# Spreading the second half's norm steps over later filler products at the border of two layers

## The chip, the cores and the metric

One core of a Trainium2 chip runs the whole program. The metric is the device time of one execution in microseconds (us); the time before is the median of three executions. The engines are named as in the profile: PE (TensorE, matrix products; PEld its weight loads), DVE (VectorE), ACT (ScalarE), POOL (GpSimd), and SP, whose queue issues every DMA.

## The reference: two decoder layers with a norm between them

The input is 1024 rows (positions) of width 1024. Layer 0 is retention, layer 1 stick-breaking attention; between them the residual stream is normed once and projected to a shared K and V, and normed again, with another gain, and projected to Q and a gate G:

```python
y = o @ ret_w_out[i]
h = h + rms_norm(y, ret_norm_post[i])
if i == N_A_LAYERS - 1:
    kv = rms_norm(h, kv_norm) @ w_kv
...
u = rms_norm(h, sb_norm_pre[j])
proj = u @ sb_w_in[j]
q, g = jnp.split(proj, [SB_QK_WIDTH], axis=-1)
```

Both projections read the same normed h; the two gains go into the weights. So at the border of the layers there is a chain: layer 0's last output y, its sum of squares over the width, `rms_norm` of y, h, the sum of squares of h, the scale of each row of h, and only then the operands of layer 1's projections.

## The kernel before: recorded operations, a planner, and filler products

**Halves.** Activations are kept transposed (width on the partitions). The 1024 positions are two halves of 512, t = 0 and t = 1. Layer 0 is finished for half 0 well before half 1, so at the border the first half's h is already normed and the second half's is not.

**Products.** Each pair of weight matrices of 1024x512 against the two halves is computed by a seven-product scheme of the Strassen kind (class `Group`, L1182): products 1 to 7, each of 4 chunks of 12 matmuls 128x128x512 into four PSUM banks, two `pma` and two `pmb` (or `pz` and `po`). A product's weight operand `whl` is a high and a low half in fp32r, made from raw fp32 weights `wraw`: ACT writes the high half (with the gain), DVE the low half, by `split` (L758). An activation operand is made in the same way: products 1 and 2 take theirs from half 0 alone, products 6, 5, 7, 3 and 4 need half 1 or both. There are three `whl` buffers, and a `whl` holds two of a product's four chunks.

**Groups and filler.** Layer 1's groups are K, Q, V0, G0, V1 and G1 (tables `kinds` and `early`, L1663 and L1664). Product 2 of the first five needs nothing of half 1 and is run ahead as filler, in that order; I call them the fillers K, Q, V0, G0 and V1. ACT copies each filler's four banks to SBUF (`f<-pma`, `f<-pmb`), and SP stores them (`s<-f`). Then come group K's product 1, product 6, 5, 7, 3, 4, and the other groups.

**The second half's chain**, recorded as side steps beside the fillers. In `a_post(1)` (L1054), `post` has 12 entries: `stat1` (four tiny matmuls, the sum over the width, then a power on POOL), `stat2` (a diagonal, `sgn`), `row` (one matmul `pz<-sgn,ones`, which spreads the scale along the positions), eight `add` steps, and `stat3`, which is `stat1` for h. An `add` step is three DVE instructions, `S<-S,gn,pz`, `S<-S,tab` and the sum of squares `acc<-acc,tab`, one ACT square `tab<-S`, and an SP store `h<-S`. `c_stats(1)` (L1117) is two entries: the diagonal and the row for h. `late` of `c_prep` (L1135) is 16 entries, four each of `rows` (half 1 times the row, four 128x512 or 128x1024 DVE instructions, and product 6's operand `xh`), `fives` (product 5's operand `qk`), `sevens` (product 7's, `oT`) and `rest` (products 3 and 4). `plain` is product 1's operands.

**What sets the order.** Nothing is issued when the Python code runs: `Recorder` notes every operation, `merge` (L693) spreads the side steps evenly over the chunks of the product they stand beside, and the record's order decides the order of the PE's work, whose turn a pooled buffer is, and the deadlines. `Plan` (L282) then goes over all recorded operations with durations per operation, and for every engine picks the next one by the time at which it can begin and the latest time at which it must be done for the PE; PE itself takes the recorded order, or a later operation among the next 100 where the recorded one would keep it waiting. The emitted program has a fixed order on each engine, and an engine that waits holds everything behind it. Because planning goes on to the end, a change in one place shifts the order in later places too.

Of the kernel before, what the change touches and what calls it, by code (L numbers as in the profile page):

```python
# [457 lines left out]
def trunk(ctx, tc, xT, wts, gains, trig, ident_in, cols, grow_in, out):  # L458
# [234 lines left out]
    def merge(main, *sides, nxt=None):  # L693


        done = [0] * len(sides)
        for i, m in enumerate(main):
            if nxt and nxt.pre and i == len(main) - 2:
                nxt.pre()
            m()  # L700
            for k, (steps, lead, tail) in enumerate(sides):
                n = len(main) - lead - tail
                upto = min(len(steps), len(steps) * max(0, i + 1 - lead) // n)
                while done[k] < upto:
                    steps[done[k]]()
                    done[k] += 1
# [20 lines left out]
    def diag(col):  # L727
        d = hl("sgn")
        for b in range(4):
            n = slice(128 * b, 128 * b + 128)  # L730
            V.tensor_scalar(d[:, 0, n], ident[:], col[:, b:b + 1], None, ALU.mult)
            V.scalar_tensor_tensor(d[:, 1, n], ident[:], col[:, b:b + 1], f32(d[:, 0, n]), ALU.mult, ALU.subtract)
        return d

    def short_row(col):
        d = S("sgn", [512])
        for b in range(4):
            n = slice(128 * b, 128 * b + 128)
            if b % 2:
                A_.activation(d[:, n], ident[:], AF.Copy, scale=col[:, b:b + 1])  # L740
            else:
                V.tensor_scalar(d[:, n], ident[:], col[:, b:b + 1], None, ALU.mult)
        return d

    def psum_row(d):
        p = PS("z")
        MM(p[:], ones[:], d[:], start=True, stop=True)
        return p

    def keep_row(d):  # L750
        p = PS("z")
        for l in range(2):
            MM(p[:], onesr[:], d[:, l, :], start=l == 0, stop=l == 1)
        row = S("acc", [512])
        A_.activation(row[:], p[:], AF.Copy)
        return row
# [297 lines left out]
    def a_post(t, y_d, acc, hold=None):  # L1054

        box = {}

        def stat1():
            box["col"] = rstd_col(acc[0])

        def stat2():
            box["d"] = short_row(box["col"]) if t else diag(box["col"])

        def row():
            box["rows"] = psum_row(box["d"]) if t else keep_row(box["d"])
            box["acc"] = S("acc", [512])

        def load(k):
            y, raw = box[k] = (hold[k % 4][:, k // 4], S("tab", [512])) if t else (S("vo", [512]), S("vo", [512]))
            if not t:  # L1070
                dma(y[:], y_d[k])
            dma(raw[:], xT[128 * k:128 * k + 128, HT * t:HT * t + HT])

        def add(k):
            c2, c = divmod(k, 2)
            y, raw = box[k]
            V.scalar_tensor_tensor(y[:], y[:], gcol(G_POST, k), box["rows"][:], ALU.mult, ALU.mult)
            (V if t else G).tensor_tensor(y[:], y[:], raw[:], ALU.add)
            dma(h_d[t][c2][:, 512 * c:512 * c + 512], y[:])

        def square(k):
            y, raw = box[k]
            if k == 0:
                A_.activation(box["acc"][:], y[:], AF.Square)
            else:
                A_.activation(raw[:], y[:], AF.Square)
                (V if t else G).tensor_tensor(box["acc"][:], box["acc"][:], raw[:], ALU.add)

        def stat3():
            colh[t] = rstd_col(box["acc"])  # L1090

        return [stat1, stat2, row] + in_turn(8, 3 if t else 0, load, add, square) + [stat3]
# [24 lines left out]
    def c_stats(t):  # L1117
        box = {}

        def dia():  # L1120
            box["d"] = short_row(colh[t]) if t else diag(colh[t])

        def row():
            rowh[t] = psum_row(box["d"]) if t else keep_row(box["d"])
        return [dia, row]
# [9 lines left out]
    def c_prep(hold):  # L1135

        X = Ctx()
        X.op = {n: [None] * 4 for n in range(1, 8)}
        X.raw = [None] * 4
        X.big = {}  # L1140

        def hi_lo(n, i, src, tag="xh"):
            if tag != "xh":
                if i == 0:
                    X.big[n] = S(tag, [4, 2, 512], F32R)
                x = X.big[n][:, i]
            else:
                x = hl("xh")
            X.op[n][i] = x
            split((x[:, 0, :], x[:, 1, :]), src)  # L1150

        def early(i, c):
            if c:
                X.raw[i] = h_rows(0, i)
            hi_lo(1 + c, i, X.raw[i][:, c])

        def rows(i):
            a, b = X.raw[i], h_rows(1, i, hold)
            t6 = S("f2", [512])
            V.tensor_tensor(a[:, 0], a[:, 0], b[:, 0], ALU.subtract)  # L1160
            V.scalar_tensor_tensor(t6[:], a[:, 0], -1.0, b[:, 1], ALU.mult, ALU.subtract)
            V.scalar_tensor_tensor(a[:, 1], t6[:], -1.0, a[:, 1], ALU.mult, ALU.subtract)
            hi_lo(6, i, t6[:])
            X.raw[i] = a, b

        def fives(i):
            hi_lo(5, i, X.raw[i][0][:, 0], "qk")

        def sevens(i):
            b = X.raw[i][1]  # L1170
            V.tensor_tensor(b[:, 0], b[:, 1], b[:, 0], ALU.subtract)
            hi_lo(7, i, b[:, 0], "oT")

        def rest(i):
            a, b = X.raw[i]
            hi_lo(3, i, b[:, 1])
            hi_lo(4, i, a[:, 1])

        return X, [lambda i=i: early(i, 1) for i in range(4)], [lambda i=i: early(i, 0) for i in range(4)], \
            [lambda f=f, i=i: f(i) for f in (rows, fives, sevens, rest) for i in range(4)]  # L1180
# [405 lines left out]
    def run():  # L1586
        pend = []

        def go(main, sides=None):

            if pend:
                m, s = pend.pop()
                merge(m, *(s() if s else []), nxt=main)
            if main is not None:
                pend.append((main, sides))
# [3 lines left out]
        def make_groups(base, kinds, X, early, keep):  # L1599
            order = [tuple(n for n in ((1, 2, 6, 5, 7, 3, 4) if at < 5 else (2, 1, 6, 5, 3, 7, 4)) if n not in early[at]) for at in range(6)]  # L1600
            return order, [Group(base + 8 * at, kind, gain, X, sets[::-1] if at % 2 and at < 5 else sets, order[at], early[at], keep[at])
                           for at, (kind, gain) in enumerate(kinds)]
# [4 lines left out]
        order, groups = make_groups(0, kinds, X, early, (True, False, True, True, False, True))  # L1607
# [29 lines left out]
        post, acc = [], []  # L1637
        for k, (t, h) in enumerate(units):
# [4 lines left out]
            if t0 == 1 and h0 == 0:  # L1643
                post = a_post(0, y_d[0], acc)
# [3 lines left out]
            if (t, h) == (1, 3):  # L1648
                hold = []
                Y, load, plain, late = c_prep(hold)  # L1650
# [9 lines left out]
        post = a_post(1, y_d[1], acc, hold)  # L1660
# [3 lines left out]
        early = ((2,), (2,), (2,), (2,), (2,), ())  # L1664
        order, groups = make_groups(64, kinds, X, early, (False, False, False, False, False, True))
        ahead_of = [(at, 2) for at in range(6) if early[at]]
        steps = [[(post[:3], 1, 0)], [(plain + post[3:], 0, 0)], [(c_stats(1), 0, 0)], [(late[:4], 0, 0)], [(late[4:12], 0, 0)]]
        for k, (at, n) in enumerate(ahead_of):
            go(groups[at].chunks(n), lambda k=k: steps[k] if k < len(steps) else [])
        P = [[CPair(t, p) for p in range(NPAIR)] for t in range(2)]  # L1670
        for at, group in enumerate(groups):
            if at < 5:
                go(group.chunks(*order[at]), (lambda: [(late[12:], 0, 16)]) if at == 0 else None)
            else:
                go(group.chunks(*order[at][:-2]))
                go(group.chunks(7), lambda: [(P[0][0].rows(0) + P[0][0].mix(0), 0, 0)])
                go(group.chunks(4), lambda: [(P[0][0].rows(1) + P[0][0].mix(1), 0, 0), (P[0][1].rows(0), 0, 0)])
# [5 lines left out]
        acc, post = [], []  # L1683
        turns, done = finish()
        for k, (t, p, hh) in enumerate(seq):
            if k < 2:
                continue
            steps = P[t][p].mix(hh)
# [15 lines left out]
            if f == (0, 3) and hh == 1:  # L1704
                post = c_post(0, y_d[0], acc)
        last = P[1][3].out(y_d[1], done=done)
        last.pre()
        merge(last)

    run()  # L1710
    end, order, start = Plan(in_turn_of_buffers(rec.ops)).best()
    with tc.manual_schedule():
# [74 lines left out]
```

## Time and profile before

| what | value |
|---|---|
| median of three executions | 1642.5 us (1640.12 to 1643.02) |
| the profiled execution's own time | 1642.06 us |
| its span, first to last instruction | 1640.2 us |
| busy share of the span: PE, PEld, DVE, ACT, POOL | 99%, 82%, 76%, 50%, 15% |
| mean granted TensorE clock | 0.997 |
| DMA | 405.88 MB, 247 GB/s over the span |

All times inside an execution are from the start of its span. A timeline row gives the start, the duration of the merged run of equal instructions (the last one's end included), engine, operation, output and inputs, count, and in brackets how long the engine was idle just before and what ended that. Nearly every instruction carries L229, the line of the recorder's `emit`, so groups are told apart by tile names. Matmuls overlap in the pipeline; what counts is the distance from one row's start to the next one's. The border of the layers lies between about 790 and 890 us.

### The profile page before, as it was taken

The page shows a single profiled execution, that of the slowest core. Times are in us where ns is not written, and L with a number is a line of the kernel's source. Part 1 is how long each engine was busy: PE and PEld are TensorE (multiplying, and loading weights), DVE is VectorE, ACT ScalarE, POOL GpSimd, SP SyncE. Part 2 cuts the span into 40 slices and gives each one's busy share as a digit, 9 for nine tenths or more (in the row PEclk, how much of TensorE's full clock was granted, in tenths as well). Part 3 has the DMA queues.
Part 4 walks back from the last instruction along what each step waited for, and adds up shares of the span by engine and source line. Part 5 has one row for each costly group of instructions (what it writes and reads, how often), then busy time and mean ns, then how long its engine had stood idle before and what let it go on. Part 6 is the DMA issues. An engine that isn't in the chain of part 4 may idle for free.

```text
span 1640.2 us, 23055 instructions
## 1 busy us (share of the span) xinstructions
PE 1623.1 (99%) x7626; PEld 1349.1 (82%) x7626; DVE 1254.1 (76%) x1954; ACT 816.0 (50%) x1496; POOL 244.9 (15%) x332
## 2 busy tenths in 40 slices
PE   8999999999999999999999999999999999999997
PEld 6888888888888888888788888888888888888886
DVE  6998679795686676767778865857747887778997
ACT  7633432322576545534565554545555655545643
POOL 0000024230022114441000000000002221212510
PEclk9999999999999999999999999999999999999999
DMA  7675636486467797798576967659686868787794
GB/s 271 242 252 174 225 115 219 154 295 225 154 246 252 261 297 266 267 309 278 200 253 221 338 227 287 245 178 321 230 314 220 272 240 301 274 283 265 266 315 147
DMA packets 200279, 405.88 MB, mean 247 GB/s; under 512 B 22496, under 2 KB 23136, under 8 KB 200160
## 3 DMA queue, kind: packets, MB, share of 16 engines
q1 hardware_dynamic: 200160, 404.42, 71.5%
q8 instruction: 60, 0.98, 0.3%
q14 instruction: 59, 0.48, 0.1%
HBM read 285.84 MB, written 118.49 MB: 247 GB/s over the span
## 4 chain that ended last, share of the span: by engine, by line
PE 76%; DVE 2%; DMA 1%; issue 0%; POOL 0%; ACT 0%; POOLq 0%; DVEq 0%; SPq 0%
PE pma L229 21%; PE pmb L229 20%; PE po L229 20%; PE pz L229 16%; DMA wraw<-in_wts_dram 1%; DVE f L229 1%; DVE wraw L229 0%; DVE S L229 0%; DVE whl L229 0%; DVE acc L229 0%; DVE small L229 0%; POOL small L229 0%; POOLq L1782 0%; ACT sgn L229 0%; DVEq L1782 0%
## 5 line engine op out<-in xcount | busy, mean ns | idle before, releaser
L229 DVE TENSOR_TENSOR whl<-wraw,whl 128x512 fp32r<-128x512 f32 x392 | 278.4, 734 | 131.5 <-ACT whl L229 130.7
L229 ACT ACTIVATE whl<-wraw 128x512 fp32r<-128x512 f32 (+1 forms) x392 | 232.8, 626 | 290.9 <-PE pmb L229 101.9
L229 PE MATMUL pmb<-oT,whl 128*128 128x512 f32 x552 | 144.7, 395 | 0.0
L229 PE MATMUL pma<-oT,whl 128*128 128x512 f32 x552 | 140.2, 395 | 0.0
L229 PE MATMUL pma<-whl,xh 128*128 128x512 f32 x456 | 119.6, 396 | 1.1 <-DVE whl L229 1.0
L229 PE MATMUL pmb<-whl,xh 128*128 128x512 f32 x456 | 117.4, 392 | 0.9 <-ACT f L229 0.9
L229 PEld LDWEIGHTS pma<-oT,whl 128*128 128x128 f32 x552 | 101.5, 188 | 20.1
L229 PEld LDWEIGHTS pmb<-oT,whl 128*128 128x128 f32 x552 | 100.8, 188 | 19.0
L229 POOL TENSOR_SCALAR_AFFINE_SELECT f<-f 128x128 f32<-128x128 f32 x64 | 31.0, 500 | 528.6 <-ACT f L229 512.3
L229 PEld LDWEIGHTS pma<-whl,xh 128*128 128x128 f32 x456 | 86.0, 190 | 19.9 <-DVE whl L229 1.8
L229 PEld LDWEIGHTS pmb<-whl,xh 128*128 128x128 f32 x456 | 86.2, 189 | 19.6 <-ACT f L229 1.5
L229 PE MATMUL pz<-ko,ko 128*128 128x512 f32 (+3 forms) x480 | 101.9, 332 | 0.0
L229 PE MATMUL pma<-xh,whl 128*128 128x512 f32 x384 | 99.1, 393 | 0.0
L229 PE MATMUL pmb<-xh,whl 128*128 128x512 f32 x384 | 98.1, 390 | 0.0
L229 POOL TENSOR_TENSOR f<-f,f 128x512 f32<-128x512 f32 x32 | 51.2, 1608 | 253.6 <-DVE f L229 226.1
L229 PE MATMUL pma<-whl,oT 128*128 128x512 f32 x312 | 82.6, 400 | 5.6 <-ACT oT L229 5.6
L229 PE MATMUL po<-xh,whl 128*128 128x512 f32 x336 | 85.3, 389 | 0.0
L229 PE MATMUL pz<-xh,whl 128*128 128x512 f32 x336 | 85.2, 389 | 0.0
L229 PEld LDWEIGHTS pz<-ko,ko 128*128 128x128 f32 x480 | 77.3, 189 | 9.2 <-DVE AT L229 0.7
L229 PEld LDWEIGHTS pma<-xh,whl 128*128 128x128 f32 x384 | 71.6, 188 | 15.4 <-ACT f L229 0.5
L229 PEld LDWEIGHTS pmb<-xh,whl 128*128 128x128 f32 x384 | 71.9, 188 | 14.9
L229 DVE SCALAR_TENSOR_TENSOR wraw<-wraw,gn,wraw 128x512 f32<-128x512 f32 x96 | 70.2, 745 | 16.4 <-DMA wraw<-in_wts_dram 8.2
(201 smaller groups left out, 3342.7 us busy)
## 6 DMA issues: line engine op xcount, KB each, us to landing
wraw<-in_wts_dram SPq DMA_DIRECT2D x559, 256.0 KB, 5.1
v<-v SPq DMA_DIRECT2D x64, 512.0 KB, 6.2
y<-f SPq DMA_DIRECT2D x112, 256.0 KB, 2.9
f<-y SPq DMA_DIRECT2D x88, 256.0 KB, 4.6
ko<-kq SPq DMA_DIRECT2D x40, 512.0 KB, 6.2
kq<-v SPq DMA_DIRECT2D x32, 512.0 KB, 6.3
s<-f SPq DMA_DIRECT2D x36, 256.0 KB, 3.3
f<-s SPq DMA_DIRECT2D x36, 256.0 KB, 4.5
```

The costliest lines, as they stand in the source:

```text
L229: f(*[_real(a) for a in o.args], **{k: _real(v) for k, v in o.kw.items()})
```

## The change: three lines in `run()`

The table `steps`, which says what is recorded beside which filler, and the tail of `late` beside group K:

```diff
-        steps = [[(post[:3], 1, 0)], [(plain + post[3:], 0, 0)], [(c_stats(1), 0, 0)], [(late[:4], 0, 0)], [(late[4:12], 0, 0)]]
+        steps = [[(post[:3], 1, 0)], [(plain + post[3:6], 0, 0)], [(post[6:9], 0, 0)], [(post[9:], 0, 0)], [(c_stats(1) + late[:2], 0, 0)]]
...
-                go(group.chunks(*order[at]), (lambda: [(late[12:], 0, 16)]) if at == 0 else None)
+                go(group.chunks(*order[at]), (lambda: [(late[2:], 0, 16)]) if at == 0 else None)
```

| recorded beside | before | after |
|---|---|---|
| filler K | stat1, stat2, row | the same |
| filler Q | plain, 8 adds, stat3 | plain, adds 1 to 3 |
| filler V0 | diagonal and row of h | adds 4 to 6 |
| filler G0 | rows 1 to 4 | adds 7 and 8, stat3 |
| filler V1 | fives, sevens | diagonal and row of h, rows 1 and 2 |
| K's products 1 and 6 | rest | rows 3 and 4, fives, sevens, rest |

No operation is added or removed; the number of instructions on each engine is the same. The planner puts them in another order. `_7546`, `_7584`, `_7602` and `_7663` are the four tiles that hold half 1 of h, two 512-wide pieces each.

DVE, from the row of y on (`pz_8086`), before. `whl_8093` and `whl_8145` are the two weight operands of filler V0; the low halves of the first stand behind the whole chain of adds, of which the last part is shown:

```order
L229 TENSOR_TENSOR acc_8117<-acc_8117,tab_7923 128x512
L229 TENSOR_TENSOR S_7663<-S_7663,tab_7944 128x512
L229 TENSOR_TENSOR acc_8117<-acc_8117,tab_7928 128x512
L229 SCALAR_TENSOR_TENSOR whl_8093<-wraw_7900,gn,whl_8093 128x512
L229 TENSOR_TENSOR acc_8117<-acc_8117,tab_7944 128x512
L229 SCALAR_TENSOR_TENSOR whl_8093<-wraw_7915,gn,whl_8093 128x512
L229 SCALAR_TENSOR_TENSOR whl_8145<-wraw_8002,gn,whl_8145 128x512
```

DVE after, from the same row on:

```order
L229 SCALAR_TENSOR_TENSOR S_7546<-S_7546,gn,pz_8086 128x512
L229 SCALAR_TENSOR_TENSOR whl_8093<-wraw_7837,gn,whl_8093 128x512
L229 SCALAR_TENSOR_TENSOR whl_8093<-wraw_7846,gn,whl_8093 128x512
L229 SCALAR_TENSOR_TENSOR S_7584<-S_7584,gn,pz_8086 128x512
L229 TENSOR_TENSOR S_7546<-S_7546,tab_7864 128x512
L229 TENSOR_TENSOR S_7584<-S_7584,tab_7874 128x512
L229 SCALAR_TENSOR_TENSOR S_7602<-S_7602,gn,pz_8086 128x512
L229 SCALAR_TENSOR_TENSOR S_7663<-S_7663,gn,pz_8086 128x512
```

The low halves of V0's first weights moved from the end of the adds to just behind the first of them.

ACT, where filler Q's four banks (`pma_8095`, `pma_8102`, `pmb_8107` and the last one) are copied out, before. The `tab` rows are the squares, each of which needs an add on DVE:

```order
L229 ACTIVATE tab_7923<-S_7584 128x512
L229 ACTIVATE f_8184<-pma_8095 128x512
L229 ACTIVATE f_8188<-pma_8102 128x512
L229 ACTIVATE tab_7928<-S_7602 128x512
L229 ACTIVATE f_8203<-pmb_8107 128x512
L229 ACTIVATE f_8205<-pmb_8115 128x512
```

ACT after, the same place:

```order
L229 ACTIVATE tab_7889<-S_7663 128x512
L229 ACTIVATE f_8176<-pma_8095 128x512
L229 ACTIVATE f_8183<-pma_8102 128x512
L229 ACTIVATE tab_7938<-S_7546 128x512
L229 ACTIVATE f_8196<-pmb_8107 128x512
L229 ACTIVATE f_8201<-pmb_8114 128x512
```

Still a square stands in front of the copies and one between them, but an earlier one of the chain: in front the fourth in place of the sixth, between them the fifth in place of the seventh.

DVE, where group K's product 1 hands its banks (`pma_8548`, after: `pma_8514`) to product 6, before. `qk` is product 5's operand:

```order
L229 TENSOR_TENSOR whl_8601<-wraw_8497,whl_8601 128x512
L229 TENSOR_TENSOR qk_8355<-S_7722,qk_8355 128x512
L229 TENSOR_TENSOR S_7546<-S_7546 128x512
L229 TENSOR_TENSOR f_8286<-pma_8548,f_8286 128x512
L229 TENSOR_TENSOR f_8306<-pma_8556,f_8306 128x512
```

DVE after, the same place. `xh_8585` and `xh_8646` are the third and fourth of product 6's four operands:

```order
L229 TENSOR_TENSOR S_7663<-S_7663,pz_8455 128x1024
L229 TENSOR_TENSOR xh_8585<-f_8578,xh_8585 128x512
L229 TENSOR_TENSOR f_8277<-pma_8514,f_8277 128x512
L229 TENSOR_TENSOR f_8285<-pma_8521,f_8285 128x512
L229 TENSOR_TENSOR f_8318<-pmb_8530,f_8318 128x512
L229 TENSOR_TENSOR f_8342<-pmb_8540,f_8342 128x512
L229 TENSOR_TENSOR whl_8593<-wraw_8445,whl_8593 128x512
```

Before, all operands of products 6 and 5 stand ahead of the hand-over; after, product 6's third is the instruction just ahead of it, and the fourth stands behind it.

## The prediction

> **What bounds the kernel now.** I read the page first, for the share of each engine, then the list of waits of PE, then PE's timeline at the border, then what DVE and ACT did there.
>
> ```profile
> span 1640.2 us, 23055 instructions
> PE 1623.1 (99%) x7626; PEld 1349.1 (82%) x7626; DVE 1254.1 (76%) x1954; ACT 816.0 (50%) x1496; POOL 244.9 (15%) x332
> PE pma L229 <- ACT oT L229: 5.6, 2, 5.2
> PE pma L229 <- DVE whl L229: 1.0, 1, 1.0
> PE pmb L229 <- ACT f L229: 0.9, 1, 0.9
> PE pma L229 <- ACT qk L229: 0.7, 1, 0.7
> ```
>
> PE is busy 99% of the span, so time is won only where PE waits or goes slower than its pace. In the list of waits (total, times, longest) the 5.6 us for `oT` are the program's start; the 1.0 for a low weight half `whl` and the 0.9 for a bank copy `f` lie at the border. They look like 1.9 us, but PE's timeline shows more:
>
> ```profile
> 798.25 0.95 PE L229 MATMUL pz<-ones,acc 128*128 128x1 f32 x8
> 799.05 1.65 PE L229 MATMUL pma<-xh,whl 128*128 128x512 f32 x6
> 804.64 1.02 PE L229 MATMUL pz<-sgn,ones 128*128 128x512 f32 x2
> 805.10 1.96 PE L229 MATMUL pma<-xh,whl 128*128 128x512 f32 x6
> 816.43 0.91 PE L229 MATMUL pma<-whl,xh 128*128 128x512 f32 x2
> 818.22 0.98 PE L229 MATMUL pmb<-whl,xh 128*128 128x512 f32 x2 [0.88 <-ACT f L229]
> 820.20 1.32 PE L229 MATMUL pma<-whl,xh 128*128 128x512 f32 x3 [1.00 <-DVE whl L229]
> 825.16 2.59 PE L229 MATMUL pma<-whl,xh 128*128 128x512 f32 x6
> 834.41 1.02 PE L229 MATMUL pz<-sgn,ones 128*128 128x512 f32 x2
> 846.20 1.52 PE L229 MATMUL pma<-whl,xh 128*128 128x512 f32 x6
> 857.08 1.52 PE L229 MATMUL pma<-xh,whl 128*128 128x512 f32 x6
> 867.96 1.52 PE L229 MATMUL pma<-xh,whl 128*128 128x512 f32 x6
> ...
> 820.00:821.00 1.00, 0.80 (x3) 0.67 (x4) 1.00 (x3) 0.77 (x2) 0.00 (x0) 0.80 0.70 250
> 821.00:822.00 1.00, 1.00 (x6) 0.90 (x5) 1.00 (x3) 0.00 (x0) 0.00 (x0) 0.50 0.81 205
> ...
> 826.00:827.00 1.00, 1.00 (x4) 0.80 (x3) 0.00 (x0) 0.00 (x0) 0.00 (x0) 0.50 1.04 402
> 827.00:828.00 1.00, 1.00 (x5) 0.82 (x4) 0.00 (x0) 0.00 (x0) 0.00 (x0) 0.79 0.77 297
> ```
>
> The starts of filler V1, product 1 and product 6 (846.20, 857.08, 867.96) lie 10.88 us apart: that is a product of 48 matmuls at full pace. The eight small matmuls of a sum over the width take 0.80 (798.25 to 799.05); a row takes 0.91, since from 804.64 to 816.43 are 11.79, and 10.88 of them are filler Q. Filler V0 with its eight small matmuls should take 11.68, but goes from 816.43 to 834.41, which is 17.98. **The border loses 6.30 us.** The windows show what the list of waits hides: the granted clock (third number from the right) is 0.80 at 820, 0.50 in each microsecond from 821 to 827, 0.79 at 827. That costs 0.20 + 6 x 0.50 + 0.21 = 3.41; six matmuls at 825.16 take about 2.4 us in place of 1.36. The other 2.89 are waits: the 1.88 in brackets, and thin issue between them.
>
> The Trainium skill, page "TensorE: Matmul & The Clock Gate", Part 1, says that the clock is halved after at least one idle window of about 3.4 us and that this window runs freely. By that the two gaps here would cost their waits alone; the trace disagrees, with half the clock after idle stretches of 0.88 and 1.00.
>
> Why PE waited stands on DVE and ACT:
>
> ```profile
> 805.70 1.41 DVE L229 SCALAR_TENSOR_TENSOR S<-S,gn,pz 128x512 f32<-128x512 f32 x2 [3.57 <-PE pz L229]
> 815.07 0.74 DVE L229 SCALAR_TENSOR_TENSOR S<-S,gn,pz 128x512 f32<-128x512 f32 x1
> 815.73 0.68 DVE L229 TENSOR_TENSOR acc<-acc,tab 128x512 f32<-128x512 f32 x1
> 816.33 0.68 DVE L229 TENSOR_TENSOR S<-S,tab 128x512 f32<-128x512 f32 x1
> 819.40 0.74 DVE L229 SCALAR_TENSOR_TENSOR whl<-wraw,gn,whl 128x512 fp32r<-128x512 f32 x1
> 820.66 2.07 DVE L229 SCALAR_TENSOR_TENSOR whl<-wraw,gn,whl 128x512 fp32r<-128x512 f32 x3
> 830.27 1.41 DVE L229 SCALAR_TENSOR_TENSOR whl<-wraw,gn,whl 128x512 fp32r<-128x512 f32 x2 [5.00 <-ACT whl L229]
> 835.47 1.22 DVE L229 TENSOR_TENSOR S<-S,pz 128x1024 f32<-128x1024 f32 x1 [3.79 <-PE pz L229]
> 836.61 1.41 DVE L229 SCALAR_TENSOR_TENSOR whl<-wraw,gn,whl 128x512 fp32r<-128x512 f32 x2
> 866.12 1.37 DVE L229 TENSOR_TENSOR f<-pma,f 128x512 f32<-128x512 f32 x2 [0.18 <-PE pma L229]
> 867.48 1.37 DVE L229 TENSOR_TENSOR f<-pmb,f 128x512 f32<-128x512 f32 x2
> ...
> 805.39 1.32 ACT L229 ACTIVATE whl<-wraw,gn 128x512 fp32r<-128x512 f32 x2
> 815.18 0.64 ACT L229 ACTIVATE tab<-S 128x512 f32<-128x512 f32 x1 [1.23 <-DVE S L229]
> 815.73 1.06 ACT L229 ACTIVATE f<-pma 128x512 f32<-128x512 f32 x2
> 817.59 1.07 ACT L229 ACTIVATE f<-pmb 128x512 f32<-128x512 f32 x2
> ```
>
> DVE got y's row at 805.70 and went through the adds. The high halves of V0's first weights were ready at 806.71 (ACT, 805.39 + 1.32), the low ones began only at 819.40, behind the adds. ACT, in order, held the bank copies behind squares that waited for DVE (1.23). Later DVE was idle 5.00 and 3.79: too much work early, too little late.
>
> **The change part by part.** Paces on DVE: 0.66 for a scalar-tensor-tensor with a gain (815.07 to 815.73), 0.60 for a tensor-tensor (815.73 to 816.33), 1.14 for the 1024-wide multiply (835.47 to 836.61), 0.68 for an add that reads PSUM (1.37 for two). So an add step is 1.86, and no work is added: what counts is who stands in front.
>
> *Filler V0.* In the new order the two low weight halves follow the first `S`: 805.70 + 3 x 0.66 = 807.7, where PE wants them at 816.43. The second pair waits for PE to free a buffer and comes before the fifth add: about 814, wanted at 816.43 + 5.44 = 821.9. The copies of Q's banks: the square between them needs the fifth add, which stands 16 DVE instructions after 805.70 (9 of 0.66, 7 of 0.60, thus 10.1), so 815.8; the square ends at 816.4, the third copy at 817.1. PE uses that bank a quarter of a chunk after another, 816.43 + 2 x 0.68 = 817.79. The spare is 0.7. So this wait goes, and with it the clock's fall: 6.30.
>
> *Filler G0* begins at 816.43 + 10.88 = 827.31; its weights and the last adds are, by the same paces, done on DVE by about 825.5. The sum for h now stands behind G0 on PE: 838.19 to 838.99, then the power on POOL and the diagonal, which fit in the 5.44 of V1's first half. The row of h stands at 844.43, 10.02 us later than before, and product 1 can begin at 844.43 + 0.91 + 5.44 = 850.78, where it was 857.08. That is again the 6.30.
>
> *Product 1 to product 6* is what is late next. DVE gets the row 1.06 after it is begun (834.41 to 835.47), at 845.5; a weight half in front, which needs a buffer that PE frees at 844.43, makes it about 846.0. Up to the hand-over stand 19 instructions: 4 x 1.14 + 3 x 0.66 + 12 x 0.60 = 13.74, so 859.8. Product 1's first bank is done at 850.78 + 8.16 + 0.68 = 859.62: DVE is just in time. The four adds out of PSUM take 2.7 to 862.5; PE wants the last of those banks at 861.66 + 2.04 = 863.70. The spare is 1.2, what it was before (first bank released at 866.80, product 6 at 867.96). Then 8 more instructions, about 5.0 us, bring product 6's fourth operand and weight: 867.5 against 861.66 + 8.16 = 869.8. Before, these were done long ahead; now they have 2.3 us. I book no loss, with DVE's backlog as the cover; each microsecond beyond 1.2 is paid in full.
>
> *SP and DMA.* Stores `h<-S` move behind weight loads, and loads of product 6 stand behind the four stores of G0's copies, which end about 839.0.
>
> ```profile
> wraw<-in_wts_dram SPq DMA_DIRECT2D x6, 256.0 KB, 5.2
> ```
>
> With this median from issue to landing (loads issued between 833 and 842) the first lands at about 844.7, and the DVE instruction that wants it stands in front of the row's multiply of 846.0: covered by 0.6 with its own 0.66. POOL has only the two powers here.
>
> *Behind the border* the planner shifts instructions again; PE's list shows no wait there that could be won or that would be lost as a rule. I take 0, and 1 us either way for the range.
>
> **The sum.** The profiled execution took 1642.06 (span 1640.2 and 1.86 around it): 1642.06 - 6.30 = 1635.76. The median is 0.44 higher, so **1636.2 us**. A measurement of this kernel can tell 0.2%, 3.3 us, from no change: faster means below 1639.2, slower above 1645.8.
>
> **The rivals.**
>
> *Part of the wait stays* (0.14). The spares of 0.7 at V0 and 1.2 at product 6 are small beside chains of 10 and 14 us. With DVE 3 us late at product 6, PE pays 1.8 without the clock's fall: 1638.0; with V0's copies late too, about 3: 1639.2. I take 1638 to 1641. For it: DVE saturated from there on. Against: the regular order on PE, which the planner shuffles where it sees an operand late (as it did in V0 before).
>
> *The clock's fall is not in the timed runs* (0.08). If it depends on where a short gap falls in the clock's window, the profiled execution may have had it and the timed ones not. Then only 2.89 are won: 1639.6. For it: the three times spread by 2.90, near 3.41. Against: the profiled execution has the fall and lies 0.44 under the median. This is the Trainium skill's rule on the free-running window, on the page named above; one trace before cannot settle it.
>
> *Gains go again behind the border* (0.06), a reordered later stage costing 4 to 6 us: 1640 to 1643. Against: the border's PE order shows that the change does what it says, and PE ran later with hardly a wait.
>
> *Slower* (0.10). The load that stands on SP behind G0's stores lands late and holds the row's multiply, with it product 6's operands and, on ACT, V1's bank copies. If DVE is 8 us late at the hand-over, PE waits 8 - 1.2 = 6.8, and the clock's fall adds 3.41: 10.2 lost for 6.3 won, 1642.5 + 3.9 = 1646.4. It decides from 4.1 us of lateness on (4.1 - 1.2 + 3.41 = 6.3), that is, from a landing after about 9.9 us in place of 5.2 on. Beyond 1645.8 it comes with 7.4 us of lateness. Against: the median of 5.2 was taken with as many loads in flight.
>
> **How the numbers follow.** The forecast has 0.62; its own range is 1636.2 less 1.5 and plus 1.6 (the shift behind the border and small waits): 1634.7 to 1637.8. Reaching to the partial and the clock's case: 1634.0 to 1641.5; that leaves out most of the slower case, part of the third and the forecast's own tails, together about 2 in 10. Faster by over 0.2%: 0.62 and half of the partial case, 0.69. Slower by over 0.2%: 0.07 of the slower case's 0.10, the rest of it being lateness between 4.1 and 7.4 us. What is left, 0.24, is within 0.2%.
>
> **What would show it.** Right: in the timeline after, V0 follows Q without a gap, the clock stays at 1.00 from 816 to 830, the sum of h stands at 838.2, product 1 begins at 850.8, product 6 at 861.7, and PE's list of waits has lost `whl` 1.0 and `f` 0.9. Wrong: a wait of PE for DVE `f` or `xh` at product 6, a wait for ACT `f` where V1 hands over, a DVE wait for DMA ahead of the row's multiply near 846, windows below 1.00 after 840, or a PE that arrives at product 6 at 861.7 and loses the time later.

## The result, and the profile after

| | before | after |
|---|---|---|
| median of 5 executions each | 1641.9 us (1639.84 to 1643.02) | 1634.66 us (1634.12 to 1636.31) |
| the profiled execution's own time | 1642.06 us | 1634.38 us |
| its span | 1640.2 us | 1632.7 us |

The ratio on record is 0.9964, with a 95% interval of 0.9954 to 0.9975 (the two medians alone give 0.9956): faster by more than 0.2%. The forecast was 1636.2 us, 1.5 above the median.

First the page after: the span, the busy shares, and then all of PE's waits that the list has (total, times, longest).

```profile
span 1632.7 us, 23067 instructions
PE 1617.7 (99%) x7626; PEld 1346.2 (82%) x7626; DVE 1251.3 (77%) x1954; ACT 813.8 (50%) x1496; POOL 245.6 (15%) x332
PE pma L229 <- ACT oT L229: 5.2, 1, 5.2
PE pma L229 <- ACT qk L229: 0.7, 1, 0.7
PE po L229 <- ACT sgn L229: 0.5, 1, 0.5
```

`whl` 1.0 and `f` 0.9 are gone, and of the 7.5 us that the span lost, 5.4 were busy time of PE, with the same 7626 matmuls: matmuls at half clock count as busy, so most of what was lost before never showed as waiting. PE's timeline after:

```profile
796.93 0.95 PE L229 MATMUL pz<-ones,acc 128*128 128x1 f32 x8
803.78 1.96 PE L229 MATMUL pma<-xh,whl 128*128 128x512 f32 x6
815.11 1.52 PE L229 MATMUL pma<-whl,xh 128*128 128x512 f32 x6
825.99 1.52 PE L229 MATMUL pma<-xh,whl 128*128 128x512 f32 x6
836.87 0.95 PE L229 MATMUL pz<-ones,acc 128*128 128x1 f32 x8
837.68 1.65 PE L229 MATMUL pma<-whl,xh 128*128 128x512 f32 x6
843.26 1.02 PE L229 MATMUL pz<-sgn,ones 128*128 128x512 f32 x2
849.61 1.52 PE L229 MATMUL pma<-xh,whl 128*128 128x512 f32 x6
860.49 1.52 PE L229 MATMUL pma<-xh,whl 128*128 128x512 f32 x6
```

Three windows of 20 us across the border (the second number is PE's busy time, the third from the right the granted clock):

```profile
800.00:820.00 20.00, 20.00 (x88) 16.19 (x87) 16.10 (x27) 12.77 (x23) 0.29 (x1) 1.00 0.76 246
820.00:840.00 20.00, 20.00 (x94) 16.67 (x93) 10.17 (x18) 12.43 (x22) 1.01 (x1) 1.00 0.95 326
840.00:860.00 20.00, 20.00 (x88) 16.19 (x87) 17.48 (x25) 13.23 (x24) 0.00 (x0) 1.00 0.71 231
```

V0 (815.11), G0 (825.99) and the sum of h (836.87) follow each other at 10.88, PE is busy in all of the 60 us, and the clock stays at 1.00. All of this stands 1.32 earlier than in before, since filler K's sum does (796.93 against 798.25). To keep that apart, I count from K's sum: product 1 begins 52.68 us behind it, and 58.83 (857.08 - 798.25) before. **The border gives 6.15 us.** From product 1 to the end of the span it is 783.1 in both (1632.7 - 849.61; 1640.2 - 857.08), so nothing was won or lost behind the border.

DVE's timeline after, first beside filler Q, then at the row of h and the hand-over:

```profile
805.05 1.41 DVE L229 SCALAR_TENSOR_TENSOR whl<-wraw,gn,whl 128x512 fp32r<-128x512 f32 x2
811.36 1.41 DVE L229 SCALAR_TENSOR_TENSOR whl<-wraw,gn,whl 128x512 fp32r<-128x512 f32 x2
813.94 0.69 DVE L229 TENSOR_TENSOR S<-S,tab 128x512 f32<-128x512 f32 x1
841.55 0.75 DVE L229 SCALAR_TENSOR_TENSOR wraw<-wraw,gn,wraw 128x512 f32<-128x512 f32 x1 [0.60 <-DMA wraw<-in_wts_dram]
844.22 0.75 DVE L229 SCALAR_TENSOR_TENSOR whl<-wraw,gn,whl 128x512 fp32r<-128x512 f32 x1 [1.92 <-ACT whl L229]
844.89 1.21 DVE L229 TENSOR_TENSOR S<-S,pz 128x1024 f32<-128x1024 f32 x1
858.65 1.37 DVE L229 TENSOR_TENSOR f<-pma,f 128x512 f32<-128x512 f32 x2
865.63 1.29 DVE L229 TENSOR_TENSOR whl<-wraw,whl 128x512 fp32r<-128x512 f32 x2
```

ACT's at the copies of filler Q's third and fourth bank:

```profile
815.20 1.07 ACT L229 ACTIVATE f<-pmb 128x512 f32<-128x512 f32 x2
```

V0's low halves now begin at 805.05 and 811.36 where the first began at 819.40; the copy that PE needs before V0's third bank begins at 815.20; and the row of h, begun on PE at 843.26, is taken at 844.89, behind the weight half at 844.22 that the forecast had put in front of it.

The other 1.32 us stand at the program's start. PE's first rows before, then after:

```profile
5.18 1.65 PE L229 MATMUL pma<-whl,oT 128*128 128x512 f32 x3 [5.18 <-ACT oT L229]
7.25 0.80 PE L229 MATMUL pma<-whl,oT 128*128 128x512 f32 x1 [0.42 <-ACT oT L229]
14.21 1.07 PE L229 MATMUL pma<-whl,oT 128*128 128x512 f32 x4
```

```profile
5.20 2.08 PE L229 MATMUL pma<-whl,oT 128*128 128x512 f32 x4 [5.20 <-ACT oT L229]
7.08 1.05 PE L229 MATMUL pmb<-whl,oT 128*128 128x512 f32 x2
12.90 1.52 PE L229 MATMUL pma<-whl,oT 128*128 128x512 f32 x6
```

The rows that begin at 14.21 and at 12.90 both open with the program's 25th matmul: 1.31 of the 1.32 are there already, 780 us ahead of the change. The run before waited 0.42 for a piece of the input and ran at half pace (0.43 us per matmul in place of 0.23) for longer.

### The profile page after: what moved, and what is told of

Its sections match the earlier page's. It is cut to its first block, busy times and chain, and to the rows that moved or that the text cites. A ratio compares the mean times of both kernels' runs of the same rounds, so it can differ in the third digit from the quotient of the medians.

```text
span 1632.7 us, 23067 instructions
## 1 busy us (share of the span) xinstructions
PE 1617.7 (99%) x7626; PEld 1346.2 (82%) x7626; DVE 1251.3 (77%) x1954; ACT 813.8 (50%) x1496; POOL 245.6 (15%) x332
## 4 chain that ended last, share of the span: by engine, by line
PE 77%; DVE 2%; issue 0%; POOL 0%; ACT 0%; POOLq 0%; DVEq 0%
PE pma L229 21%; PE pmb L229 21%; PE po L229 20%; PE pz L229 16%; DVE f L229 1%; DVE whl L229 0%; DVE wraw L229 0%; DVE small L229 0%; POOL small L229 0%; POOLq L1782 0%; ACT sgn L229 0%; DVEq L1782 0%; ACT qk L229 0%; POOL col L229 0%; DVEq L229 0%
## 5 line engine op out<-in xcount | busy, mean ns | idle before, releaser
L229 PE MATMUL pmb<-whl,oT 128*128 128x512 f32 x312 | 81.5, 396 | 0.0
```

Source lines behind the costliest of these rows:

```text
L229: f(*[_real(a) for a in o.args], **{k: _real(v) for k, v in o.kw.items()})
```

## The experiments

All were compared with runs of the kernel before on the same chip, whose medians were 1640.5 to 1640.8 us.

**1. The chain one filler later in place of two.** The adds and `stat3` stand over Q and V0; the diagonal and the row of h stand beside G0 and the first four `rows` beside V1, one filler earlier than in after. Against after:

```diff
-        steps = [[(post[:3], 1, 0)], [(plain + post[3:6], 0, 0)], [(post[6:9], 0, 0)], [(post[9:], 0, 0)], [(c_stats(1) + late[:2], 0, 0)]]
+        steps = [[(post[:3], 1, 0)], [(plain + post[3:7], 0, 0)], [(post[7:], 0, 0)], [(c_stats(1), 0, 0)], [(late[:4], 0, 0)]]
...
-                go(group.chunks(*order[at]), (lambda: [(late[2:], 0, 16)]) if at == 0 else None)
+                go(group.chunks(*order[at]), (lambda: [(late[4:], 0, 16)]) if at == 0 else None)
```

> Adds 1 to 4 beside filler Q, 5 to 8 and the sum of h beside V0, the diagonal and row beside G0, rows 1 to 4 beside V1, the rest beside K: the chain is one filler later than in the kernel before, where the changed kernel has it two later. Theory A (the gain is that V0's low weight halves and Q's bank copies no longer stand behind the adds on DVE): the first low halves again stand behind the first add, so the 6.2 us at V0 are won in full and the median is that of the changed kernel, 1634.7 within 1.5. Rival B (the gain needs the rows and operands moved behind V1): a good part of the 6.2 is missing, 1638 or more.

Measured: 1635.63 us, ratio 0.9970 (0.9959 to 0.9982), span 1634.0. PE's list has the same three waits as after, and from K's sum to product 1 it takes 52.68 to the hundredth. Neither the sum so late (behind G0) nor the row beside V1 is needed.

**2. The tail alone is moved**, against before:

```diff
-        steps = [[(post[:3], 1, 0)], [(plain + post[3:], 0, 0)], [(c_stats(1), 0, 0)], [(late[:4], 0, 0)], [(late[4:12], 0, 0)]]
+        steps = [[(post[:3], 1, 0)], [(plain + post[3:], 0, 0)], [], [], [(c_stats(1) + late[:2], 0, 0)]]
...
-                go(group.chunks(*order[at]), (lambda: [(late[12:], 0, 16)]) if at == 0 else None)
+                go(group.chunks(*order[at]), (lambda: [(late[2:], 0, 16)]) if at == 0 else None)
```

> All adds and the sum of h beside filler Q as in the kernel before; diagonal, row and first operands beside V1 and K as in the changed one. Theory A: the low halves of V0's weights stand behind the adds again, PE waits at V0 and the clock halves: about 1641 (1640 to 1642.5), with windows at 0.50 near 821 to 827. Rival B: the gain comes from the later rows and operands: 1634.7 to 1637.

Measured: 1641.49 us, ratio 1.0004 (0.9994 to 1.0013). PE at V0:

```profile
816.36 0.98 PE L229 MATMUL pmb<-whl,xh 128*128 128x512 f32 x2 [0.87 <-ACT f L229]
818.34 1.65 PE L229 MATMUL pma<-whl,xh 128*128 128x512 f32 x3 [1.00 <-DVE whl L229]
```

Two windows of 1 us there:

```profile
817.00:818.00 1.00, 0.34 (x1) 0.03 (x1) 1.00 (x3) 0.95 (x2) 0.00 (x0) 0.85 0.89 285
818.00:819.00 1.00, 0.66 (x2) 0.57 (x3) 1.00 (x3) 0.91 (x2) 0.00 (x0) 0.50 1.06 293
```

The two waits are as before, the clock falls at about 817.7 and is at 0.50 for some 6.8 us, and V0 with its sum takes 17.70 (814.56 to 832.26) where 11.83 would do. The tail's move alone does nothing.

**3. The sum late, the adds not.** All eight adds stay beside Q as in before, and `stat3` moves to G0; the diagonal, the row and `late` stand as in after. Against after:

```diff
-        steps = [[(post[:3], 1, 0)], [(plain + post[3:6], 0, 0)], [(post[6:9], 0, 0)], [(post[9:], 0, 0)], [(c_stats(1) + late[:2], 0, 0)]]
+        steps = [[(post[:3], 1, 0)], [(plain + post[3:11], 0, 0)], [], [(post[11:], 0, 0)], [(c_stats(1) + late[:2], 0, 0)]]
```

> All adds recorded beside filler Q as in the kernel before, only the sum of h recorded beside G0 (and the diagonal, row and operands after it as in the changed kernel). Theory A1 (the place of the sum's matmuls on PE sets the adds' deadline, and the deadline, not the place in the record, put the adds ahead of the weights): 1634.7 within 1.5, no wait at V0. Rival A2 (the adds have to be recorded beside later fillers): a wait at V0 as before, about 1641.

Measured: 1635.53 us, ratio 0.9968 (0.9955 to 0.9980), and 52.68 from K's sum to product 1. DVE's low halves for V0:

```profile
806.25 1.41 DVE L229 SCALAR_TENSOR_TENSOR whl<-wraw,gn,whl 128x512 fp32r<-128x512 f32 x2
812.56 1.41 DVE L229 SCALAR_TENSOR_TENSOR whl<-wraw,gn,whl 128x512 fp32r<-128x512 f32 x2
```

They stand where they stand in after (1.2 later, as K's sum does), although every add is recorded beside Q again. So it is not the adds' place in the record that puts the weights behind them, but the place of the sum that the adds feed.

**4. One step moved.** That suggests the smallest change: `stat3` one filler later, all else as in before:

```diff
-        steps = [[(post[:3], 1, 0)], [(plain + post[3:], 0, 0)], [(c_stats(1), 0, 0)], [(late[:4], 0, 0)], [(late[4:12], 0, 0)]]
+        steps = [[(post[:3], 1, 0)], [(plain + post[3:11], 0, 0)], [(post[11:] + c_stats(1), 0, 0)], [(late[:4], 0, 0)], [(late[4:12], 0, 0)]]
```

> The kernel before with one step moved: `stat3`, the last entry of `post`, goes from filler Q to filler V0, where the diagonal and the row of h follow it; the adds, the rows, fives and sevens stay where they were. Theory A1 (the border's loss comes from the place of h's sum on PE: recorded at the end of Q, it gives the whole chain of adds a deadline ahead of V0's weights): V0 follows Q without a gap, the sum stands in the middle of V0 and costs its 0.80 there, `whl` 1.0 and `f` 0.9 leave PE's list of waits, and the time is that of after, 1634.7 within 1.0. Rival E (the whole spread over V0, G0 and V1 is needed; with the row still wanted by V0's end, DVE is late for G0's weights or for the sum): waits of 1 us or more between 815 and 840, with or without half the clock, 1636.5 to 1641.

Measured: 1635.53 us, ratio 0.9970 (0.9958 to 0.9981). PE at the sum of h, and product 1's first row:

```profile
821.76 1.02 PE L229 MATMUL pz<-ones,acc 128*128 128x1 f32 x8 [0.20 <-DVE acc L229]
850.88 1.52 PE L229 MATMUL pma<-xh,whl 128*128 128x512 f32 x6
```

From K's sum (797.78) to product 1 it is 53.10: 5.73 of the 6.15 us come with this one entry. What is left is the sum's wait for the last add, 0.20, and the pause around it. The clock did not fall at it.

**5. The row of h half a product later.** The diagonal and the row have V1 to themselves, so that the row stands at V1's end; all of `late` goes beside group K's products. Against after:

```diff
-... [(c_stats(1) + late[:2], 0, 0)]]
+... [(c_stats(1), 0, 0)]]
...
-                go(group.chunks(*order[at]), (lambda: [(late[2:], 0, 16)]) if at == 0 else None)
+                go(group.chunks(*order[at]), (lambda: [(late, 0, 16)]) if at == 0 else None)
```

> As the changed kernel, but the row of h at the end of filler V1 in place of its middle, 5.44 us later, and all four rows beside K's product 1. Theory A with the spare as predicted (1.2 us at the hand-over to product 6, 2.3 at its last operand): PE loses 3 to 4 us at product 6, and 3.4 more if the clock halves, so 1638 to 1642, with PE waiting for DVE f, xh or whl. Rival C (DVE's order leaves enough room, the spare is over 5.4 us): 1634.7 within 1.5.

Measured: 1635.0 us, ratio 0.9966 (0.9954 to 0.9979). On PE the row stands 51.78 behind K's sum, where it was 46.33: 5.45 us later. Product 6 still begins 63.56 behind K's sum, as in after. DVE:

```profile
846.09 2.98 DVE L229 SCALAR_TENSOR_TENSOR wraw<-wraw,gn,wraw 128x512 f32<-128x512 f32 x4
850.29 2.35 DVE L229 TENSOR_TENSOR S<-S,pz 128x1024 f32<-128x1024 f32 x2 [1.23 <-PE pz L229]
867.61 0.69 DVE L229 TENSOR_TENSOR xh<-f,xh 128x512 fp32r<-128x512 f32 x1
```

The planner put sums of weights, which after's DVE does partly behind the row, in front of it (846.09), and DVE even waits 1.23 for the row. So the rival's time came, though not by room in after's order: the order changed. Product 6's fourth operand is done at 868.2; PE wants it at 861.02 + 8.16 = 869.18.

**6. The row inside product 1.** The diagonal and the row go beside K's product 1 as well, with `rows`. Against after:

```diff
-        steps = ... [(post[9:], 0, 0)], [(c_stats(1) + late[:2], 0, 0)]]
+        steps = ... [(post[9:], 0, 0)]]
...
-                go(group.chunks(*order[at]), (lambda: [(late[2:], 0, 16)]) if at == 0 else None)
+                go(group.chunks(*order[at]), (lambda: [(c_stats(1) + late[:4], 1, 20), (late[4:], 3, 16)]) if at == 0 else None)
```

> The border as in after up to the end of the adds, but the diagonal, the row of h and the four `rows` steps are recorded beside group K's product 1, so that the row stands inside product 1 on PE: some 11 us later than in after. Theory C2 (moving the row later costs nothing only as long as DVE still has product 6's operands by their turn): the first of them would be ready about 861.8 against 861.0 wanted, the fourth about 873 against 869, so PE shows waits for DVE `xh` or `f` between 860 and 875 of about 4 us in sum, and if the clock falls there as at the border of before, 3.4 more: 1638.5 to 1642. Rival D2 (the planner can always put other work in front, on PE too): no wait over 1 us there, 1634.7 within 1.5.

Measured: 1636.39 us, ratio 0.9973 (0.9965 to 0.9982), 1.7 above after's median. PE in product 6:

```profile
861.86 1.92 PE L229 MATMUL pma<-xh,whl 128*128 128x512 f32 x6
864.30 0.39 PE L229 MATMUL pz<-qk,whl 128*128 128x512 f32 x1
869.12 0.73 PE L229 MATMUL pma<-xh,whl 128*128 128x512 f32 x2 [0.34 <-ACT xh L229]
```

Here the cover ends, but gently: the planner lets PE take four matmuls of product 5 (`qk`) between those of product 6, the one wait is 0.34, and the clock stays at 1.00. From product 6's start to where product 5 follows it whole, PE has lost 1.33 us against after, and 1.83 up to the end. Neither time expected was right, the rival's by little (it had no wait over 1 us, which held, and 1634.7 within 1.5): the loss begins where I said, at a third of its size.

**7. The kernel before, once more.**

> The kernel before, unchanged, for one more profile. Theory A (the waits at filler V0 always take the clock with them): V0 with its sum takes 17.7 to 18.0 from the first of its rows to the next sum, and the 1-us windows show 0.50 for 6 to 7 us from about 3 us after V0's start. Rival B2 (the clock falls only when the gaps meet its window in a certain way): V0 takes 14.3 to 14.8 and the windows stay at or near 1.00. The span: 1640.2 within 2 by A, 1637 within 2 by B2.

Measured: span 1641.4. PE at V0:

```profile
817.51 0.92 PE L229 MATMUL pma<-whl,xh 128*128 128x512 f32 x2
821.28 1.36 PE L229 MATMUL pma<-whl,xh 128*128 128x512 f32 x3 [0.99 <-DVE whl L229]
835.50 1.02 PE L229 MATMUL pz<-sgn,ones 128*128 128x512 f32 x2
```

V0 takes 17.99, where it took 17.98, with six windows at 0.50 again. Every profile of a kernel with the sum beside Q has the clock's fall at the border; none of the others has.

The timed executions show that it is not there every time. The record has the mean granted clock of each: 0.998 or 0.999 in all 47 executions of the kernels whose profiles have no fall at the border. A whole fall takes 3.41 of some 1640 us off, 0.002, so that 0.997 is the most that can be read with it. Yet 13 of the 44 executions of before that were run beside the experiments have 0.998; their median is 1639.5 us, that of the other 31 is 1641.2. In experiment 2 it is 3 of 11, with 1639.1 against 1641.7. In these executions the fall was missing or shorter; which of the two is not shown, since none of them was profiled. Theory A's *always* does not hold.

**8. The changed kernel, once more.**

> The changed kernel, unchanged, for a second profile. If the whole difference between profiles of one border lies at the start: from the sum beside filler K to product 1 52.7 again, from product 1 to the end 783.1 within 0.7, and the span differs from 1632.7 by as much as the 25th matmul's start differs from 12.90.

Measured: span 1635.6, time 1637.35. PE's 25th matmul, K's sum and product 1:

```profile
14.87 1.52 PE L229 MATMUL pma<-whl,oT 128*128 128x512 f32 x6
799.79 0.95 PE L229 MATMUL pz<-ones,acc 128*128 128x1 f32 x8
852.47 1.52 PE L229 MATMUL pma<-xh,whl 128*128 128x512 f32 x6
```

The border is the same 52.68, and from product 1 to the end 783.1. Of the 2.9 us that this execution is longer, 1.97 are there at the 25th matmul; the other 0.89 come before K's sum, nearly all of it by 60 us (one and the same row begins at 59.29 here and at 56.53 in after, 2.76 apart), and part of it is a wait of 0.36 at 56 us, so that the expectation holds for the border and not wholly for the start.

**9. PE made busy at the start**, to see whether the pace there can be had earlier. The nine products' result is used by nothing:

```diff
     V.memset(ones[:], 1.0)
+    warmup = PS("z")
+    for _ in range(9):
+        MM(warmup[:, :128], ones[:], ones[:], start=True, stop=True)
```

> After, with nine 128x128x128 matmuls of the constant matrix `ones` with itself at the program's start, in a bank that nothing reads; all of the reference is still computed. Theory S (1.3 of the 7.5 us between the two profiled spans, and most of the 2 to 3 us by which runs of one kernel differ, come from how long the clock stays at half after PE's first work): PE works from about 1.1 us on in place of 5.2, so the clock's ramp begins earlier; the rows show about 0.23 us per matmul 128x128x512 from 6 to 8 us on in place of 9.6 to 11.9; each microsecond less at half clock is 0.5 won, so 1.5 to 2.5 us: 1632.2 to 1633.2, with the runs within 1.5 of each other. Rival T (the slow first rows are their operands arriving late, or the clock starts to rise at a fixed time of the program): 1634.7 within 0.8, the same spread.

Measured: 1634.83 us (1633.88 to 1636.54), ratio 0.9962 (0.9949 to 0.9976): after's time, with after's spread. In its profiled execution the second piece of the input landed late. PE:

```profile
8.59 0.50 PE L229 MATMUL pma<-whl,oT 128*128 128x512 f32 x1 [2.05 <-ACT oT L229]
```

And two windows behind that wait:

```profile
9.00:10.00 1.00, 1.00 (x5) 0.79 (x4) 0.48 (x2) 1.00 (x3) 0.00 (x0) 0.82 1.02 387
10.00:11.00 1.00, 1.00 (x4) 0.79 (x3) 0.72 (x2) 1.00 (x3) 0.00 (x0) 0.50 1.03 389
```

The matmuls were at full pace at 8.9 us, but the gap of 2.05 took the clock to 0.50 from about 9.6 to 13.0. So a second profile:

> The kernel with nine products of `ones` with itself at the start, once more, for a second profile. If the late landing of the second piece of the input was chance there (PE waited 2.05 for it, until 8.59), this profile has matmuls of 0.23 from 5.2 us on, no wait over 0.5 behind the first, and the 25th matmul before 11.5 us, where it began at 12.90 in after and at 15.10 with the late landing; the span is then about 1631.5. If a faster PE only comes sooner to operands that have not landed, the 25th matmul stands at 12 us or later whatever the pace.

Measured: span 1632.2. PE:

```profile
5.23 1.32 PE L229 MATMUL pma<-whl,oT 128*128 128x512 f32 x4
8.72 0.73 PE L229 MATMUL pma<-whl,oT 128*128 128x512 f32 x2 [0.36 <-ACT whl L229]
11.58 1.52 PE L229 MATMUL pma<-whl,oT 128*128 128x512 f32 x6
```

With the input in time, four matmuls take 1.32 where they took 2.08, so the pace can be had; the 25th matmul stands at 11.58, between the two expectations, since PE now comes to weights that are not there (0.36). In the median nothing of it is left: theory S's 1632.2 to 1633.2 did not come, and the time and the spread are those of rival T. Of a version that is faster than the changed kernel I have no evidence.

## Why the prediction was right

*The border's size.* Forecast 6.30, measured 6.15. All of the chain came out: with the start's 1.32 taken off, V0 was to begin at 815.11, G0 at 825.99, the sum of h at 836.87, product 1 at 849.46 and product 6 at 860.34; they began at 815.11, 825.99, 836.87, 849.61 and 860.49. The 0.15 is a mis-sized term: I reckoned a filler with its eight small matmuls at 11.68, but the six matmuls behind them take 1.48 (837.68 to 839.16) in place of 1.36, which before's rows showed as well (1.65 at 799.05). The border should have been put at 17.98 - 11.83 = 6.15.

*V0's operands.* The second pair of low halves was to be done at about 814, less 1.32, and was (811.36 + 1.41); the fifth add's `S` at 815.8, less 1.32, and was at 814.5; the third bank's copy begins at 815.20, with the spare of 0.7. But why they are in time was only half said: I spoke of who stands in front on DVE, and took the spreading of the adds as what changes it. Experiments 3 and 4 show that the place of `stat3` decides it. The reason is read from the planner's code, where `limits` works the latest time of every instruction back from the matmuls that need it: beside Q, the matmuls of `stat3` give the adds a deadline ahead of V0's weights. The deadlines themselves stand in no run.

*Product 1 to product 6.* DVE's instants came out within 0.3 of the forecast (row multiplied from 844.89, hand-over at 858.65, product 6's last weight at 866.2). **The step that failed is the price behind them, "each microsecond beyond 1.2 is paid in full".** It supposes a fixed order, and the planner does not keep it: with the row 5.45 us later nothing was lost, and with it some 11 us later 1.8. A term for lateness in a planned program needs the new order.

*The load on SP.* It was to land at 844.7 with 0.6 of cover, less 1.32. DVE's last wait for a load in front of the row ends at 841.55: about 2 us earlier. The slower rival needed it 4.7 us later than forecast (9.9 in place of 5.2). That a load lands late in an execution, which no planner can foresee, was not tried.

*The clock's fall.* The rival said that it could be missing from the timed runs, with 2.89 won. The medians differ by 7.2 (by the interval 4.1 to 7.6), which leaves 2.89 out, and the profiles of experiments 2 and 7 have the fall again with 3.4. But the rival held in part: 13 of 44 executions of before cannot have had the whole of it (experiment 7), and so it is, by their shorter times, one cause of the spread of before's times. The start is another: the changed kernel, without any fall at its border, spreads by 2.2 in five executions and by 2.9 between two profiles, nearly all of it from the first 60 us. That the median fell by more than the border's 6.15 is taken for chance, since the 44 executions have a median of 1640.8, 6.2 above that of after.

*Behind the border* nothing was won or lost (0 forecast, 0.03 measured). *The start* I had not foreseen: the profile of before and that of after differ there by 1.32 by chance: that is most of the 1.38 by which the profiled execution came out below the 1635.76 that was reckoned for it.

## What to carry to other kernels

Where a planner orders work by deadlines, look for what sets the deadline: here one tiny reduction, recorded a filler too early, pulled a chain of 24 DVE instructions ahead of weights that were needed sooner, and one entry of a table gives 5.7 of 6.15 us. Read PE's loss from the distance between row starts and from windows of the clock, since waits of 1.9 us cost 6.15 and most of that counted as busy. And before a difference of some us between two profiles is explained, find a mark ahead of the change (here the sum beside filler K) and take off what differs there already.

## What the runs showed of the hardware

*Short gaps can take the clock.* In three profiles (before, experiments 2 and 7) two gaps of 0.87 to 1.00 us, with 1 us of work between them, brought the granted clock to 0.50 for 6.8 us; one gap of 2.05 us brought it there for 3.4 (experiment 9); single gaps of 0.74 (experiment 3, at 55 us), 0.36 (experiment 8) and 0.20 (experiment 4) did not. In 13 of 44 timed executions of before the mean granted clock, 0.998, leaves no room for the whole 6.8 us, so the same two gaps need not have the same price each time. The Trainium skill, page "TensorE: Matmul & The Clock Gate", Part 1, has windows of 3.4 us that run freely, and half the clock after at least one idle window. The durations agree, one window and two; the idle part does not, since no window here was idle as a whole: in experiment 2 PE was busy for 0.34 and 0.66 of the two microseconds around the fall.

*The clock at the start.* In the profiles without the added products, matmuls ran at 0.43 us each from about 5.2 us until between about 8.7 (experiment 2) and 12.7 (experiment 7), another time in each; with the landing of the input and a wait of up to 0.74 near 55 us this is most of what profiles of one and the same border differ by. The Trainium skill, page "TensorE: Matmul & The Clock Gate", Part 1, has full clock after one busy window; as the window runs freely, that gives 3.4 to 6.8 us of half pace behind the first matmul, as an estimate (one window to two). By the rows, experiment 2 (3.5 us), after (until about 9.8, 4.6 us) and experiment 1 (until about 11.4, 6.2 us) lie within it; experiments 8 and 7, with waits of 0.70 and 1.60 for the input before 8.3 us (until about 12.6 and 12.7), lie beyond. The granted clock in the windows does not show it:

```profile
6.00:7.00 1.00, 1.00 (x3) 0.81 (x3) 0.42 (x1) 0.29 (x1) 0.00 (x0) 1.00 0.70 246
```

This window of after reads 1.00 and has three matmuls begun, where 12:13 of the same profile has six. At a program's start the pace of the rows is to be read, and not that column.
